# A decoder layer in 32-bit products: the border inside its second feed-forward, the loads ahead of its mixer's output, and its opening, ordered anew

## The chip, the cores and the metric

The kernel runs on one core of one Trainium2 chip. The metric is the time of one execution on the device in microseconds (us). The three runs of the kernel before lie within 0.62 us of each other.

## The reference

One layer of a decoder, batch 1, 1024 tokens and 16 meta tokens ahead of them, width 1024, feed-forward width 2816, all in float32. Cut to what matters:

```
h = h + 0.5 * swiglu(rms_norm(h, ffn1_norm), ffn1_w_in, ffn1_w_out)
u = rms_norm(h, mix_norm) @ w_in
o = concat(hgrn2(u[...]), stick_breaking(u[...]))
h = h + o @ w_out
h = h + 0.5 * swiglu(rms_norm(h, ffn2_norm), ffn2_w_in, ffn2_w_out)
return h without the padding and the meta tokens

def swiglu(h, w_in, w_out):
    g, u = split(h @ w_in, 2)
    return (silu(g) * u) @ w_out
```

## The kernel before

Every large product is made of three matmuls. A float32 operand is split into a rounded high part and the rest: ScalarE casts the high part (`wh`, `xh`, `th`), VectorE subtracts it from the source to get the low part (`wl`, `xl`, `tl`), and TensorE adds up high by high, low by high and high by low. The two feed-forwards save products besides, by Winograd's form of Strassen's scheme: operands are cut into two by two blocks, and sums and differences of blocks (operands T1 to T4 on the side of the activations, s1, s2 and so on the side of the weights) are multiplied instead of the blocks alone.

The stages run one after the other: first feed-forward in and out, row norm and projection `w_in`, the HGRN2 heads and the attention woven into each other, the product with `w_out` in two halves (first the half whose operand `oT` comes back from memory, `first_half_of_o`; then the half from `oH`), the row norm with its transposes ("turns"), and the second feed-forward in and out. TensorE's order is written out by hand (`manual_schedule`). The order on the other engines comes from a scheduler, which puts work under `high_priority` ahead and holds work under `issue_after(x)` until x has been issued. All loads are issued by SP, in one order; a load waits on SP for the tile it overwrites and for its queue lane (there are eight), and all loads behind it wait too. Pools are regions of the on-chip memory: a pool that opens where another was must wait for the last use of what lay there.

The product into the feed-forward is `fast_in` (from L255). For each pair of 128 feature columns it runs two quads (gate and up). A quad loads four weight blocks (`block`, L275), makes their sums on GpSimd, splits them (`operand`, L270 and L272) and does seven groups of twelve matmuls into the banks qa, qb, qc (L315), in the order B11, T2, B21, T3, T1, T4, B22 of the operands on the other side. The gate goes through Silu; gate times up is stored to memory as `act` (four blocks B11 to B22, L427), and GpSimd makes the four sums T1 to T4 from them (`combined`, L442 and L449) and stores them too. For the last pair of the second feed-forward `combined` is put aside in `self.late`.

The first 272 tokens of the first feed-forward don't go through Strassen's scheme: they are "plain" (banks qd), run first, while the other two thirds of the tokens are loaded, normed (`norm_rows`, L645 to L665), turned and made into operands (`first_block`, `first_combined`). That opening starts with the rows of x (L614 to L617), the squares on ScalarE (L660) and VectorE (L656), root, reciprocal, scaling (L661 to L665), the transposes (L642) and the plain operand X (L674, L675). VectorE and GpSimd also build masks there: a memset, two selects on GpSimd (L112, L116) and a cast (L120) per level, one `sd` tile for all levels.

The product out of the feed-forward is `fast_out` (from L486): seven steps (A12, A11, S1, S2, S4, S3, A22), each over eleven quarters q, each of twelve matmuls (L593). A quarter loads a block of w_out (`raw`, L503, 256 KB) and one of act (L508, 256 KB) through the pool `ring`, and splits both into the pool `parts` (L513 and L515, four buffers). After quarter 3 of A12 `load_h` loads the eight residual rows hN (512 KB each, L1772), into which the steps' results are added. At quarter 2 of A12 the hook `between` runs the late `combined`.

Between the two products of the second feed-forward, the pools wq and xs_b (operands T2, T3, T1, T4, B22 in that order, 16 KB a partition each) close, and ring, parts and h3 (hN) open in that order on the same memory, from the bottom up. So the ring (24 KB) lies over wq, which holds the split weight blocks, and the beginning of T2; parts (32 KB) lie over T2, T3 and the beginning of T1; hN over T1, T4 and B22.

Of the kernel before, what the change touches and what calls it, by code (L numbers as in the profile page):

```python
# [34 lines left out]
def drain(gen):  # L35
    for _ in gen:
        pass


class Block:  # L40
# [53 lines left out]
    def setup_rest(self, pool):  # L94
# [32 lines left out]
        nc.vector.tensor_sub(mx, l0, l1)  # L127
        nc.scalar.activation(self.lb, mx, AF.Sigmoid)
        nc.scalar.activation(self.lbc, mx, AF.Sigmoid, scale=-1.0)

# [124 lines left out]
    def fast_in(self, ops, n, w_in, actD, openers, ev0, open_ev, feed=None, plain=None,  # L255
# [71 lines left out]
        def plain_quad(col, take):  # L327
            for i in range(2):
                ps = None
                for h in range(2):  # L330
                    ps = alone(ps, operand(block(i, h, col)), h, h == 0)
                    if h == 1:
                        take(i, ps)
                    yield
# [65 lines left out]
        def pair(f, opened=None, also=(None, None)):  # L400
# [17 lines left out]
            def up(i, j, ps, plus):  # L418
                t = sg[i, j]
                if plus is None:  # L420
                    nc.vector.tensor_mul(t, ps, t)  # L421
                else:
                    u = ev["p"].tile([P, n], F32, tag="u", name="u", bufs=2)
                    nc.vector.tensor_add(u, ps, plus)
                    nc.vector.tensor_mul(t, u, t)
                if (i, j) != (0, 1):
                    nc.gpsimd.dma_start(actD[f // 2, f"B{i + 1}{j + 1}"], t)  # L427
                elif self.late is None or f // 2 < D_FF // 256 - 1:
                    combined()
                else:  # L430
                    self.late.append(combined)

            def combined():
# [11 lines left out]
                t1 = made(sg[0, 1], sg[0, 0])  # L445
                put("T1", t1)
                t2 = made(sg[1, 1], t1)
                put("T2", t2)
                sub(sg[0, 1], sg[1, 1], sg[0, 1])  # L449
                put("T3", sg[0, 1])  # L450
                put("T4", made(sg[1, 0], t2))

# [33 lines left out]
    def fast_out(self, out_of, n, w_out, actD, load_h, ready, between=lambda a, q: None,  # L486
# [90 lines left out]
        for bank, a, b, start, (i, j) in steps:  # L577
# [4 lines left out]
            for q in range(nq):  # L582
                with ExitStack() as first:
                    if a == "A12" and q < 2 and not plain:
                        first.enter_context(self.tc.high_priority())
                    wh, wl = halved(left(a, q), "w", 512)
                    xh, xl = halved(right((q, b), n), "t", n)
                order = [(m, e) for m in range(nb) for e in range(3)]
                if a == "A12" and q == 0:
# [162 lines left out]
    def hgrn_fill(self, xh, xl, pool, dst):  # L752

        nc = self.nc
        plan = [(kind, h) for h in range(4) for kind in "vfqg"]
        first = {"v": 1024, "f": 512, "q": 0, "g": 1536}
# [572 lines left out]
    def run(self):  # L1329
# [20 lines left out]
        with ExitStack() as c0:  # L1350
            with ExitStack() as c1:
                with tc.manual_schedule(engines={nc.tensor.engine}), ExitStack() as c2:
# [39 lines left out]
                    for _ in self.first_block(2, rows[1], rp, "ba", ops, ba):  # L1392
                        next(steps)
                    rows.append(self.rows_of(1, rp, nc.sync))
                    self.norm_rows(1, rows[2], junk)
                    drain(islice(steps, 4))
                    for _ in self.first_block(1, rows[2], rp, "bb", None, bb):
                        next(steps)
                    for _ in self.first_combined(ba, bb, ops, rp, nw):
                        next(steps)  # L1400
                    drain(steps)
# [199 lines left out]
            with tc.manual_schedule(engines={nc.tensor.engine}):  # L1601
                right, cx, pre = ExitStack(), ExitStack(), ExitStack()
                with ExitStack() as c1:
# [11 lines left out]
                    def from_dram(b):  # L1615
                        t = self.pool_o.tile([P, 2, 4, P], F32R, tag="oT", name="oT", bufs=3)
                        for i in range(2):
                            nc.sync.dma_start(
                                t.bitcast(F32)[:, i],
# [41 lines left out]

                    for b in range(2):
                        begin(0, b)
                    ws[1] = self.mix_weights(0, 1)
                    xa = self.pool("xs_a", ctx=right, side="right")
# [38 lines left out]
                    for at, (_, f) in enumerate(self.mix_out(  # L1704
# [5 lines left out]
                        if at % 4 == 3 and i:  # L1710
                            next(turns[b])
                            due.append((at + 7, turns[b]))
                        if due and due[0][0] <= at:
                            next(due.pop(0)[1])
                self.wq = self.pool("wq", ctx=cx)
                xb = self.pool("xs_b", ctx=cx)
                operands(xb, ("T2", "T3", "T1", "T4", "B22"))
                self.pin = self.pool("pin2", 1, PSUM, cx)
# [33 lines left out]
                cx.close()  # L1752
                with ExitStack() as c1:
                    self.ring = self.pool("ring", ctx=c1)
                    self.parts = self.pool("parts", ctx=c1)
                    self.pout = self.pool("pout2", 1, PSUM, c1)
                    hN = self.pool("h3", ctx=c1).tile([P, KT, D], F32, name="hN3")

# [10 lines left out]

                    def load_h():  # L1770
                        for b in range(KT):
                            nc.sync.dma_start(hN[:, b, :], h2N[b])  # L1772

                    def between(step, q):
                        if step == "A12" and q == 2:
                            self.late.pop()()
                            right.close()

                    self.op = lambda: self.pool("op", ctx=c1, side="right")
                    self.ring_bufs = 6  # L1780
                    self.fast_out(out_of, n, a["ffn2_w_out"][0], actD, load_h, ready, between)

# [22 lines left out]
```

## Time and profile before

| | us |
|---|---|
| median of 3 runs | 2097.42 (2096.95 to 2097.57) |
| the profiled execution | 2094.55 |
| its span | 2092.8 |
| TensorE busy in it | 2013.8 (96%) |
| VectorE busy | 1380.0 (66%) |
| ScalarE busy | 903.9 (43%) |
| GpSimd busy | 632.2 (30%) |
| mean granted TensorE clock | 0.993 |

In the profile PE is TensorE's matmuls and PEld its weight loads, DVE is VectorE, ACT ScalarE, POOL GpSimd, SP the engine that issues the loads. A row of the timeline has the start, the duration, the engine, the line of the kernel, the operation, what it writes and reads, how many in succession were merged (x2), and in brackets how long the engine was idle before and what released it. A granted clock below 1 means that TensorE ran at a lower speed in a part of the stretch.

### The profile page before, as it was taken

The numbers are of one execution on the slowest core, as the hardware profiler recorded it, in microseconds if no ns is written. First come the engines' busy times: TensorE is split into PE (matmuls) and PEld (weight loads), VectorE is DVE, ScalarE is ACT, GpSimd is POOL, SyncE is SP. The second block draws the span as 40 slices with busy tenths as digits, with TensorE's granted clock in tenths as the row PEclk, the third lists the DMA queues.
The fourth block names the chain that finished last, engine by engine and source line by source line (L and its number), as shares of the span: only waits on it lengthen the run. The fifth ranks groups of instructions, "written<-read, shape, count | busy, mean of one in ns | idle before, by whom it ended". The sixth has DMA issues, their size and how long they took to land.

```text
span 2092.8 us, 31593 instructions
## 1 busy us (share of the span) xinstructions
PE 2013.8 (96%) x11249; PEld 1788.4 (85%) x11249; DVE 1380.0 (66%) x2073; ACT 903.9 (43%) x1859; POOL 632.2 (30%) x692
## 2 busy tenths in 40 slices
PE   7999999999999999999999998999999999989998
PEld 6999999999987899988887887787788888867887
DVE  6867745556788832367788676558676676656874
ACT  7633333334564534356666515145233233224443
POOL 2256635442000002253333201112564454530000
PEclk9999999999999999999999999999999999999999
DMA  7643322327875636344444154763332332348563
GB/s 216 203 141 109 114 83 90 102 73 236 289 230 178 207 108 198 131 135 117 127 131 127 49 198 142 237 210 111 111 106 91 106 115 92 101 176 304 169 226 111
DMA packets 287534, 313.90 MB, mean 150 GB/s; under 512 B 24016, under 2 KB 215888, under 8 KB 287376
## 3 DMA queue, kind: packets, MB, share of 16 engines
q1 hardware_dynamic: 270192, 259.78, 39.9%
q0 software_dynamic: 16144, 52.10, 6.5%
q8 instruction: 89, 1.46, 0.3%
q14 instruction: 69, 0.57, 0.1%
q10 hardware_dynamic: 1040, 0.00, 0.0%
HBM read 227.57 MB, written 84.23 MB: 149 GB/s over the span
## 4 chain that ended last, share of the span: by engine, by line
PE 77%; DVE 5%; ACT 2%; DMA 2%; issue 2%; POOL 0%; SPq 0%; DVEq 0%; ACTq 0%; POOLq 0%
PE o L593 17%; PE qb L315 13%; PE qc L315 8%; PE qa L315 8%; PE proj L164 5%; PE proj L162 5%; PE proj L163 5%; PE qd L315 3%; PE o L556 3%; PE wo L1244 3%; PE flip L1063 2%; PE lvl L832 2%; DVE keep L1209 1%; PE oacc L1133 1%; PE oacc L1135 1%
## 5 line engine op out<-in xcount | busy, mean ns | idle before, releaser
L315 PE MATMUL qb<-T,wh 128*128 128x384 f32 (+1 forms) x1056 | 319.5, 363 | 6.9 <-DVE u L359 6.8
L272 DVE TENSOR_TENSOR wl<-s,wh 128x512 fp32r<-128x512 f32 x176 | 200.1, 1137 | 96.5 <-ACT wh L270 92.4
L315 PEld LDWEIGHTS qb<-T,wh 128*128 128x128 f32 x1056 | 195.8, 188 | 31.8 <-ACT wh L270 9.2
L593 PE MATMUL o<-wh,th 128*128 128x512 f32 x539 | 212.3, 396 | 9.7 <-ACT th L513 9.7
L315 PE MATMUL qa<-B,wh 128*128 128x384 f32 (+1 forms) x704 | 214.8, 367 | 2.2 <-DVE sg L421 1.4
L593 PE MATMUL o<-wl,th 128*128 128x512 f32 x539 | 211.2, 394 | 0.9 <-DVE wl L515 0.9
L593 PE MATMUL o<-wh,tl 128*128 128x512 f32 x539 | 211.1, 393 | 0.7 <-DVE tl L515 0.7
L272 DVE TENSOR_TENSOR wl<-raw,wh 128x512 fp32r<-128x512 f32 x184 | 172.2, 938 | 53.6 <-ACT wh L270 49.9
L162 PE MATMUL proj<-xh,wh 128*128 128x384 f32 (+2 forms) x576 | 204.9, 356 | 0.2 <-ACT xh L252 0.2
L270 ACT CAST wh<-s 128x512 fp32r<-128x512 f32 x176 | 109.3, 622 | 220.0 <-PE qb L315 171.4
L163 PE MATMUL proj<-xh,wl 128*128 128x384 f32 (+2 forms) x576 | 199.2, 346 | 0.0
L164 PE MATMUL proj<-xl,wh 128*128 128x384 f32 (+2 forms) x576 | 198.9, 345 | 0.1
L270 ACT CAST wh<-raw 128x512 fp32r<-128x512 f32 x184 | 113.4, 619 | 198.1 <-PE qc L315 106.6
L315 PE MATMUL qb<-T,wl 128*128 128x384 f32 (+1 forms) x528 | 191.9, 363 | 1.3 <-DVE wl L272 1.3
L513 ACT CAST th<-act 128x512 fp32r<-128x512 f32 (+2 forms) x176 | 96.8, 550 | 186.8 <-PE o L593 138.9
L315 PE MATMUL qd<-X,wh 128*128 128x272 f32 x704 | 146.3, 294 | 5.8 <-ACT wh L270 4.9
L515 DVE TENSOR_TENSOR tl<-act,th 128x512 fp32r<-128x512 f32 (+2 forms) x176 | 105.1, 600 | 64.8 <-ACT th L513 64.7
L315 PEld LDWEIGHTS qa<-B,wh 128*128 128x128 f32 x704 | 130.4, 188 | 19.2 <-DVE sg L421 1.8
L285 POOL TENSOR_TENSOR s<-raw 128x512 f32<-128x512 f32 x88 | 119.2, 1354 | 82.1 <-DVE wl L272 65.4
L1209 DVE TENSOR_TENSOR_SCAN keep<-keep 128x144 f32<-128x144 f32 (+6 forms) x112 | 127.2, 1138 | 8.3 <-ACT keep L1205 6.0
L1214 POOL TENSOR_TENSOR sig<-sig,keep 128x144 f32<-128x144 f32 (+3 forms) x64 | 88.1, 1377 | 141.8 <-DVE keep L1209 79.3
L315 PE MATMUL qa<-B,wl 128*128 128x384 f32 (+1 forms) x352 | 128.7, 366 | 0.4 <-DVE wl L272 0.4
(340 smaller groups left out, 4767.4 us busy)
## 6 DMA issues: line engine op xcount, KB each, us to landing
raw<-in_ffn_w_in_dram SPq DMA_DIRECT2D x224, 256.0 KB, 3.0
raw<-in_ffn_w_out_dram SPq DMA_DIRECT2D x176, 256.0 KB, 4.2
raw<-in_w_in_dram SPq DMA_DIRECT2D x28, 512.0 KB, 4.4
ks<-kD SPq DMA_DIRECT2D x32, 260.0 KB, 5.5
oT<-oD SPq DMA_DIRECT2D x32, 256.0 KB, 4.8
ak<-in_ffn_w_out_dram SPq DMA_DIRECT2D x22, 256.0 KB, 4.9
v<-vD SPq DMA_DIRECT2D x8, 576.0 KB, 4.7
vD<-vhl SPq DMA_DIRECT2D x8, 512.0 KB, 3.6
```

What stands on the lines that cost most here:

```text
L162: nc.tensor.matmul(ps, wh[:, s], xs, start=k == 0, stop=False)
L163: nc.tensor.matmul(ps, wl[:, s], xs, start=False, stop=False)
L164: nc.tensor.matmul(ps, wh[:, s], xl[:, k, c0 : c0 + n], start=False, stop=k == nk - 1)
L270: nc.scalar.copy(hi, src)
L272: nc.vector.tensor_sub(lo, src, hi.bitcast(F32))
L285: op(t, x, y)
L315: nc.tensor.matmul(ps, a[:, k, :], b[:, k0 + k, :], start=start and k == 0 and i == 0, stop=k == 3 and i == 2, skip_group_check=True,)
L513: nc.scalar.copy(hi, src)
L515: nc.vector.tensor_sub(lo, src, hi.bitcast(F32))
L593: nc.tensor.matmul(banks[bank][m], z[:, m * P : (m + 1) * P], y, start=start and q == 0 and e == 0, stop=q == nq - 1 and e == 2, skip_grou ...
L1209: nc.vector.tensor_tensor_scan(out=kv, data0=kv, data1=kv, initial=1.0 if last else keep[:, end : end + 1], op0=ALU.mult, op1=ALU.bypass,)
L1214: nc.gpsimd.tensor_mul(sig, sig, keep[:, 1 : nk + 1])
```

## The change

Six edits.

The operands of the second feed-forward are allocated in the order B22, T4, T1, T3, T2 instead of T2, T3, T1, T4, B22, so the ones read last lie lowest. The pools of the product out open in the order h3, parts, ring instead of ring, parts, h3: hN (32 KB a partition) comes to lie over wq and B22, a new tile `spare` (24 KB) over T4 and part of T1, parts (32 KB) over the rest of T1 and T3, the ring (24 KB) over T2 and free memory.

`load_h` does nothing there any more; the hook `between` issues one residual row at each of the quarters 3 to 10 of A12. `combined` yields after each of its sums; the late one is begun one sum at a time at the quarters 2 to 5, each behind a one-column copy on GpSimd (into `spare`) that reads the newest low part `tl`. Everywhere else it is drained at once.

In the mixer, the loads of the first two rows hm and of four blocks of w_out (`ws[1]`) are held until the last oT load has been issued. The turns of the norm come one k step (three matmuls) later.

In the opening, the plain quads' operands, with their loads, get high priority; the two sigmoids of the mixer's bounds move in the code to the HGRN2 heads; and the plain steps are dealt out among the other thirds' transposes in another rhythm.

```diff
@@ plain_quad
-                    ps = alone(ps, operand(block(i, h, col)), h, h == 0)
+                    with self.tc.high_priority():
+                        w = operand(block(i, h, col))
+                    ps = alone(ps, w, h, h == 0)
@@ up
-                    combined()
+                    drain(combined())
@@ combined: a yield behind put("T1"), put("T2") and put("T3")
@@ fast_out
+                self.newest = xl
@@ the opening
                     for _ in self.first_block(2, rows[1], rp, "ba", ops, ba):
-                        next(steps)
+                        drain(islice(steps, 2))
...
-                    drain(islice(steps, 4))
                     for _ in self.first_block(1, rows[2], rp, "bb", None, bb):
-                        next(steps)
-                    for _ in self.first_combined(ba, bb, ops, rp, nw):
-                        next(steps)
+                        drain(islice(steps, 2))
+                    for at, _ in enumerate(self.first_combined(ba, bb, ops, rp, nw)):
+                        if at % 5 < 4:
+                            next(steps)
@@ from_dram
-                            nc.sync.dma_start(
+                            self.last_o = nc.sync.dma_start(
@@ the mixer's second half
-                    for b in range(2):
-                        begin(0, b)
-                    ws[1] = self.mix_weights(0, 1)
+                    with tc.issue_after(self.last_o.ins):
+                        for b in range(2):
+                            begin(0, b)
+                        ws[1] = self.mix_weights(0, 1)
...
-                            due.append((at + 7, turns[b]))
+                            due.append((at + 8, turns[b]))
...
-                operands(xb, ("T2", "T3", "T1", "T4", "B22"))
+                operands(xb, ("B22", "T4", "T1", "T3", "T2"))
@@ the second product out
+                    ph = self.pool("h3", ctx=c1)
+                    hN = ph.tile([P, KT, D], F32, name="hN3")
+                    spare = ph.tile([P, 3, 2, D], F32, name="spare")
+                    self.parts = self.pool("parts", ctx=c1)
                     self.ring = self.pool("ring", ctx=c1)
-                    self.parts = self.pool("parts", ctx=c1)
                     self.pout = self.pool("pout2", 1, PSUM, c1)
-                    hN = self.pool("h3", ctx=c1).tile([P, KT, D], F32, name="hN3")
...
-                    def load_h():
-                        for b in range(KT):
-                            nc.sync.dma_start(hN[:, b, :], h2N[b])
+                    held = []
 
                     def between(step, q):
-                        if step == "A12" and q == 2:
-                            self.late.pop()()
+                        if step != "A12":
+                            return
+                        if q >= 3:
+                            nc.sync.dma_start(hN[:, q - 3, :], h2N[q - 3])
+                        if q == 1:
+                            held.append(self.late.pop()())
+                        if 2 <= q <= 5:
+                            mark = nc.gpsimd.tensor_copy(
+                                spare[:, 0, 0, q : q + 1], self.newest[:, 0:1].bitcast(F32)
+                            )
+                            with tc.issue_after(mark.ins):
+                                next(held[0], None)
+                        if q == 5:
+                            drain(held[0])
                             right.close()
```

**The border on SP.** Rows of SP from the first load of the second product out, with what each waits for; raw is a block of w_out, act one of the activations, hN a residual row, DMAHW and DMASW are queue lanes. Before:

```order
L503 DMA raw<-in_ffn_w_out_dram 128x512 [waits DVE_49,PE_49]
L503 DMA raw<-in_ffn_w_out_dram 128x512
L508 DMA act<-act0B_13833 128x512 [waits DMAHW5_49,DMASW6_49,Pool_49]
L508 DMA act<-act1B_13840 128x512 [waits DMAHW6_49,DMASW4_49]
L503 DMA raw<-in_ffn_w_out_dram 128x512 [waits DMAHW7_49]
L508 DMA act<-act2B_13847 128x512 [waits DMAHW0_49,DMASW3_49]
L503 DMA raw<-in_ffn_w_out_dram 128x512 [waits DMAHW1_49]
L508 DMA act<-act3B_13854 128x512 [waits DMAHW2_49,DMASW2_49]
L1772 DMA hN_19221<-h2N 128x1024 [waits DMAHW3_49,DMASW1_49,DMASW0_49]
L1772 DMA hN_19221<-h2N 128x1024 [waits DMAHW4_49]
```

Now:

```order
L506 DMA raw<-in_ffn_w_out_dram 128x512 [waits PE_49]
L506 DMA raw<-in_ffn_w_out_dram 128x512
L511 DMA act<-act0B_13833 128x512 [waits DMAHW5_49,DMASW6_49]
L511 DMA act<-act1B_13840 128x512 [waits DMAHW6_49,DMASW4_49]
L506 DMA raw<-in_ffn_w_out_dram 128x512 [waits DMAHW7_49,PE_49]
L511 DMA act<-act2B_13847 128x512 [waits DMAHW0_49,DMASW3_49]
L506 DMA raw<-in_ffn_w_out_dram 128x512 [waits DMAHW1_49]
L511 DMA act<-act3B_13854 128x512 [waits DMAHW2_49,DMASW2_49]
L1785 DMA hN_19212<-h2N 128x1024 [waits DMAHW3_49,DVE_49,PE_49]
L506 DMA raw<-in_ffn_w_out_dram 128x512 [waits DMAHW4_49]
L511 DMA act<-act4B_13861 128x512 [waits DMAHW5_49,DMASW1_49]
L1785 DMA hN_19212<-h2N 128x1024 [waits DMAHW6_49]
```

The first eight loads no longer wait for VectorE or GpSimd, and the residual rows, eight in a run before, stand one between each two blocks; the first of them carries the wait for the memory of B22.

**The mixer on SP.** Rows of SP up to the last oT load; res are rows of the residual, KB a block of the HGRN2 heads, raw here a block of w_out. Before:

```order
L1656 DMA hm<-hmN 128x1024
L1618 DMA oT<-oD 128x4x128
L907 DMA KB<-hg_g 128x1024
L1626 DMA res<-h1N 128x512
L1618 DMA oT<-oD 128x4x128 x3
L1656 DMA hm<-hmN 128x1024
L1626 DMA res<-h1N 128x512
L1618 DMA oT<-oD 128x4x128 x2
```

Now:

```order
L1624 DMA oT<-oD 128x4x128 x2
L913 DMA KB<-hg_g 128x1024
L1632 DMA res<-h1N 128x512
L1624 DMA oT<-oD 128x4x128 x2
L1632 DMA res<-h1N 128x512
L1624 DMA oT<-oD 128x4x128 x2
L1632 DMA res<-h1N 128x512
L1624 DMA oT<-oD 128x4x128 x2
L1662 DMA hm<-hmN 128x1024 x2
```

The hm rows, 512 KB each, have moved from between the oT loads to behind the last of them.

**The opening on VectorE.** Its rows from the second memset of the masks on; ss_x holds the sums of squares, row the rows of x. Before:

```order
L664 RECIPROCAL ss_x<-ss_x 128x1
L656 SCALAR_TENSOR_TENSOR junk_229,ss_x<-row 128x1024
L665 TENSOR_SCALAR row<-row,ss_x 128x1024
L664 RECIPROCAL ss_x<-ss_x 128x1
L99 CAST ident_b<-ident 128x128
L665 TENSOR_SCALAR row<-row,ss_x 128x1024
L120 CAST masks<-sd 128x128
```

Now:

```order
L99 CAST ident_b<-ident 128x128
L120 CAST masks<-sd 128x128
L107 MEMSET sd 128x128
L111 MEMSET sd 128x32x2
L120 CAST masks<-sd 128x128
L107 MEMSET sd 128x128
L111 MEMSET sd 128x16x4
L120 CAST masks<-sd 128x128
L107 MEMSET sd 128x128
L111 MEMSET sd 128x8x8
```

Two more rounds follow in the same way (a cast, two memsets, a cast, a memset), and only then the first reciprocal: five levels of the masks stand ahead of the norm's first step on VectorE, none before. On SP the first row there is now the load of eight blocks of ffn_w_in, ahead of the four loads of the first rows of x, which came first before.

More of the change, by code (lines that the diff above doesn't have):

```diff
@@ L127, in setup_rest @@
         nc.vector.tensor_sub(mx, l0, l1)
-        nc.scalar.activation(self.lb, mx, AF.Sigmoid)
-        nc.scalar.activation(self.lbc, mx, AF.Sigmoid, scale=-1.0)
     def weights(self, name, raw, split, ctx, on_vector=False):
@@ L446, in combined @@
                 put("T1", t1)
+                yield
                 t2 = made(sg[1, 1], t1)
                 put("T2", t2)
+                yield
                 sub(sg[0, 1], sg[1, 1], sg[0, 1])
                 put("T3", sg[0, 1])
+                yield
                 put("T4", made(sg[1, 0], t2))
@@ L754, in hgrn_fill @@
         nc = self.nc
+        nc.scalar.activation(self.lb, self.mx, AF.Sigmoid)
+        nc.scalar.activation(self.lbc, self.mx, AF.Sigmoid, scale=-1.0)
         plan = [(kind, h) for h in range(4) for kind in "vfqg"]
@@ L1780, in run @@
                     self.ring_bufs = 6
-                    self.fast_out(out_of, n, a["ffn2_w_out"][0], actD, load_h, ready, between)
+                    self.fast_out(out_of, n, a["ffn2_w_out"][0], actD, lambda: None, ready, between)
 NAMES = [
```

## The prediction

> **What bounds the kernel now.** I read the page first. Its first part says that TensorE is busy nearly throughout, so only time in which TensorE waits, or runs at half clock after a wait, can be won.
>
> ```profile
> span 2092.8 us, 31593 instructions
> PE 2013.8 (96%) x11249; PEld 1788.4 (85%) x11249; DVE 1380.0 (66%) x2073; ACT 903.9 (43%) x1859; POOL 632.2 (30%) x692
> ```
>
> The profiled execution took 2094.55 us, 1.75 more than its span and 2.87 less than the median of 2097.42; I make the sum against 2094.55 and add 2.87 at the end. Then the waits of TensorE, asked for in the stretches that the change touches. Columns: who waits for whom, total us, times, longest.
>
> ```profile
> PE xps L642 <- DVE ss_x L664: 8.9, 1, 8.9
> PE qd L315 <- ACT wh L270: 4.9, 1, 4.9
> ...
> PE wo L1244 <- DMA oT<-oD: 4.1, 2, 3.7
> PE turn L247 <- DVE xn L240: 1.2, 1, 1.2
> ...
> PE o L593 <- ACT th L513: 9.7, 2, 6.3
> ```
>
> The largest, 9.7, stands between the two products of the second feed-forward. Third, the same stretches by windows: length, busy time and count of PE, PEld, DVE, ACT and POOL, granted clock, DMA share, GB/s.
>
> ```profile
> 0.00:14.43 14.43, 4.61 (x25) 4.20 (x25) 7.05 (x24) 7.76 (x17) 5.44 (x10) 1.00 0.94 287
> 37.80:48.00 10.20, 5.21 (x23) 4.68 (x22) 6.45 (x17) 8.50 (x17) 0.00 (x0) 0.67 0.28 72
> 1340.00:1362.00 22.00, 17.86 (x90) 13.96 (x89) 8.57 (x18) 3.04 (x7) 2.16 (x4) 0.92 0.95 307
> 1428.00:1456.00 28.00, 24.56 (x105) 18.82 (x105) 27.49 (x41) 23.08 (x43) 5.85 (x5) 1.00 0.44 123
> 1845.00:1862.00 17.00, 17.00 (x76) 13.80 (x74) 7.57 (x11) 2.97 (x5) 2.94 (x4) 1.00 0.08 32
> 1862.00:1874.00 12.00, 5.68 (x14) 4.31 (x14) 9.80 (x10) 4.95 (x8) 7.30 (x8) 0.72 0.91 325
> 1874.00:1892.00 18.00, 14.58 (x53) 11.46 (x52) 5.50 (x10) 5.67 (x10) 0.00 (x0) 0.81 1.04 412
> ```
>
> In the 17 us before the border the DMA engines move 32 GB/s and ScalarE works 3 us; in the 12 us after it everything is wanted at once. Where the clock column is below 1, a half clock lasted twice (1 - clock) of the stretch: 6.7 us from 1862 on, 6.8 from 1874 on, 3.5 in 1340 to 1362, 6.7 in 37.8 to 48.
>
> **The border of the second feed-forward.** Its timeline:
>
> ```profile
> 1845.60 0.39 PE L315 MATMUL qb<-T,wh 128*128 128x512 f32 x1
> ...
> 1861.83 0.39 PE L315 MATMUL qc<-B,wh 128*128 128x512 f32 x1
> 1862.25 0.84 SPq L503 DMA_DIRECT2D raw<-in_ffn_w_out_dram  x2
> ...
> 1862.98 0.69 DVE L425 TENSOR_TENSOR sg<-u,sg 128x512 f32<-128x512 f32 x1
> ...
> 1864.94 0.62 ACT L513 CAST wh<-raw 128x512 fp32r<-128x512 f32 x1 [10.17 <-DMA raw<-in_ffn_w_out_dram]
> ...
> 1865.59 3.93 DVE L515 TENSOR_TENSOR wl<-raw,wh 128x512 fp32r<-128x512 f32 x2 [1.92 <-ACT wh L513]
> ...
> 1866.03 6.14 SPq L1772 DMA_DIRECT2D hN<-h2N  x8
> ...
> 1868.53 2.07 PE L593 MATMUL o<-wh,th 128*128 128x512 f32 x4 [6.32 <-ACT th L513]
> ...
> 1869.44 1.28 DVE L515 TENSOR_TENSOR tl<-act,th 128x512 fp32r<-128x512 f32 x2
> ...
> 1873.82 0.53 PE L593 MATMUL o<-wh,th 128*128 128x512 f32 x1
> ...
> 1874.13 0.33 SPq L503 DMA_DIRECT2D raw<-in_ffn_w_out_dram  x1
> ...
> 1884.45 0.62 ACT L513 CAST wh<-raw 128x512 fp32r<-128x512 f32 x1 [11.97 <-DMA raw<-in_ffn_w_out_dram]
> ...
> 1885.74 0.80 PE L593 MATMUL o<-wh,th 128*128 128x512 f32 x1 [3.42 <-ACT th L513]
> ```
>
> The ring lies over the split weights' pool, so the first load of the second product goes out at 1862.25, when the last matmul (1861.83) has read them. TensorE waits 6.32; its first twelve matmuls then take 5.29 (1868.53 to 1873.82), against twelve times 0.23 in the stretch before it (17.00 us for 76 starts is 0.224 each): 2.6 lost to the clock. Behind the fourth weight block SP issues eight residual rows of 512 KB, so the fifth block goes out at 1874.13 and its split starts at 1884.45: a second wait of 3.42, and of the 6.8 us of half clock some 5.4 fall behind 1885.74 and cost half, 2.7. Together 6.3 + 2.6 + 3.4 + 2.7 = 15.0.
>
> After the change the ring of loads lies over T2, whose last reads are the twelve matmuls from 1845.60 on, so they end near 1848.4, and the splits' pool lies over T1 and T3, free by about 1856.5. Four weight blocks and four act blocks (2 MB, 6.5 us at 325 GB/s) land by about 1856, through a DMA that was idle. ScalarE is idle too and has 8 casts of 0.62 to do, 5 us, by 1862. VectorE does not get there: its rows put the first wl behind the sg of 1862.98 (end 1863.67), so wl comes at 1864.3, a second wl follows, and tl at 1865.7. TensorE has four matmuls on wh and th (to 1863.0), waits 1.3, has four on wl (to 1865.3), waits 0.4. So 1.7 is left of 15.0. The second wait: at quarter q (2.73 us of work each) SP now sends one row of 512 KB, then 512 KB of weight and act: 1 MB, 3.2 us at 325, 2.5 at 412. Quarter 4 lands near 1865.5 and is wanted at 1874.8; each further one loses 0.5, so quarter 10 still comes 5 us early. Cover gone, this would cost the 6.1 of before. The four held sums cost VectorE: two wl took 3.93 beside GpSimd's sums, two tl 1.28 alone, so a sum holds VectorE some 1.3. One sum a quarter makes 1.28 + 1.3 = 2.6 of 2.73: hidden, barely; not hidden, 0 to 3 in all. Term: **-13.3**, between -9 (sums and one more wait exposed) and -15.
>
> The Trainium skill ("SBUF — State Buffer", section "SBUF: two separate sides") says that VectorE, with two operands in SBUF, and a GpSimd instruction take one pair of ports, and that the loser is blocked for the whole instruction; the 3.93 against 1.28 agrees, and by that rule the term is the same.
>
> **The loads ahead of the mixer's last oT.**
>
> ```profile
> 1349.16 0.43 SPq L1656 DMA_DIRECT2D hm<-hmN  x1
> ...
> 1351.14 3.02 SPq L1618 DMA_DIRECT2D oT<-oD  x3
> ...
> 1359.26 1.22 PE L1244 MATMUL wo<-wh,oT 128*128 128x512 f32 x2 [3.67 <-DMA oT<-oD]
> ```
>
> The oT that ends the 3.67 is issued at 1351.14 behind an hm of 512 KB, in a DMA at 0.95 share. The change sends hm and two w_out blocks, 512 KB more, behind the last oT: 1 MB out of the way, 1.7 us at 307 GB/s for each half. If only hm counts the wait is 2.0, if both 0.3; I take 0.9, since the DMA is full throughout. A wait that short has not cost the clock elsewhere (the stretch from 1428 has a granted 1.00 with TensorE idle 3.4 in all), so the 2.8 us of half clock after 1359.26 (1.4 lost) goes too. Before 4.1 + 1.4 = 5.5, after 0.9: **-4.6**, between -2 and -5.5. hm and the held blocks are wanted only when the half of w_out from oH runs, some 20 us later.
>
> **Turns one step later.** A step is three matmuls, 0.7 us, against the wait of 1.2 for xn: **-0.7**, between 0 and -1.4.
>
> **Operand pools reversed at the start of the second feed-forward.** VectorE is busy 27.49 of 28: splits and turns are the bound whatever lies where, and T2 now waits for the last row's norm, which its own cast came after anyway. **0**, between -1.5 and +1.5.
>
> **The opening.**
>
> ```profile
> 2.48 0.71 POOL L116 TENSOR_SCALAR_AFFINE_SELECT sd<-sd 128x128 f32<-128x128 f32 x1
> 2.65 6.49 SPq L277 DMA_DIRECT2D raw<-in_ffn_w_in_dram  x8
> 5.31 1.06 ACT L660 ACTIVATE junk<-row 128x1024 bf16<-128x1024 f32 x1 [2.52 <-DMA row<-in_x_dram]
> ...
> 8.03 0.75 DVE L665 TENSOR_SCALAR row<-row,ss_x 128x1024 f32<-128x1024 f32 x1
> ...
> 8.88 4.61 PE L642 MATMUL xps<-ident,row 128*128 128x128 f32 x24 [8.88 <-DVE ss_x L664]
> ...
> 10.36 2.74 POOL L112 TENSOR_SCALAR_AFFINE_SELECT sd<-sd 128x128 f32<-128x128 f32 x1 [7.17 <-DVE sd L111]
> ...
> 14.43 0.59 PE L315 MATMUL qd<-X,wh 128*128 128x272 f32 x1 [0.94 <-DVE X L675]
> ...
> 42.95 0.60 PE L315 MATMUL qd<-X,wh 128*128 128x272 f32 x1 [4.86 <-ACT wh L270]
> ...
> 91.62 0.34 PE L315 MATMUL qa<-B,wh 128*128 128x384 f32 x1
> ```
>
> High priority takes the plain splits' loads along: eight blocks of 256 KB now go out ahead of the first rows of x. 2 MB and the first row at 287 GB/s from about 2 us end near 11, where the first row was squared from 5.31 on: about 6 late. VectorE meanwhile does four more rounds of the masks ahead of the first reciprocal, each two selects of 0.71 and a cast and memsets on VectorE that hand over to each other, some 2.2 by estimate: from 3.4 to about 12.3, as late as the row itself. From the row's scaling (8.03) to the first plain matmul (14.43) it was 6.4 and stays so: 14 + 6.4 = 20.5, **+6.1**, bounds +4.5 and, with each select at 2.74, +20. What it buys: the plain splits no longer stand behind the blocks of the other thirds on ScalarE and VectorE, so the wait of 4.86 goes, and with it half of the 5.0 us of half clock after 42.95, 2.5: -7.4. The plain stretch ends with the qa of 91.62:
>
> ```profile
> 14.43:91.62 77.19, 70.88 (x528) 69.40 (x529) 62.93 (x135) 60.26 (x119) 15.40 (x22) 0.96 0.59 174
> ```
>
> VectorE's 63 us of work in it now have 71 instead of 77, and the rows of the other thirds come later, so I allow +0.3 of new waits. Term: **-1.0**, between -4 and +6.
>
> [...]
>
> The sums that are no longer made at once elsewhere (drain) change nothing.
>
> **Sum.** -13.3 - 4.6 - 0.7 + 0 - 1.0 = -19.6. 2094.55 - 19.6 = 2075.0 profiled, 2077.8 as a median.
>
> **Rivals.**
> The opening loses: the rows of x, late behind the weights, make TensorE wait again for the B operands near 91, or the masks run longer: net +5 to +8 there instead of -1, total -11 to -14, 2083.5 to 2086.5. For it: VectorE's 8 us of slack are all it has. Against: 4.86 and 2.5 are there to win. 0.17.
> The second border wait stays: residual rows between the blocks fill the DMA (3.2 us a quarter against 2.73) and with the late sums' stores the lead of 5 to 9 us is eaten. +6, 2084. Against: 412 GB/s were reached there. 0.08.
> The oT wait stays, since the backlog at 0.95 share is of other loads and stores. Then -0.5 instead of -4.6: 2082. 0.08.
> Slower: the opening's mask rounds at 2.74 a select. Five rounds of 6 us end near 33, the first plain matmul comes at 40, +18 net, about 2097; it decides from a first plain matmul later than 41, where nothing of the other 18.6 is left. Against it: a select took 0.71 when VectorE was quiet, and it is quiet there. 0.02, with another 0.02 for just about no change.
> The change doing nothing at all can't be: the rows of SP differ in all three places.
>
> **How the numbers follow.** Forecast 0.65 at 2077.8, its own terms within 2072 and 2082. The other cases reach up to 2086.5. Range 2071 to 2086.5; below it the bounds all at their best (1 in 20), above it border and opening failing together. Measurement tells about 0.2%, 4.2 us, from no change: faster by more 0.96, same 0.02, slower 0.02.
>
> **What would show it.** Right: the first w_out load near 1848 less what was won before, one wait of 1 to 2 for wl (VectorE) at the border instead of 6.3 for th, none of 3.4 after it, no granted clock below 1 there; oT's wait below 2; the first plain matmul near 20 and no 4.9 wait behind it; the first qa at 88 to 92. Wrong: a first qa after 96, a wait for th or wh in the border's quarters 4 to 10, or 3 us of oT.

## The result, and the profile after

The changed kernel takes 2080.35 us in the median of 4 runs (2077.59 to 2080.70); the kernel before took 2097.49 in the median of the 4 runs beside it (2096.95 to 2099.33). The ratio is 0.9914, 95% interval 0.9897 to 0.9931: 17 us less, where 19.6 had been forecast. The profiled execution took 2077.59 with a span of 2075.9, against a span of 2092.8: 16.9 less.

The waits of TensorE, in the same stretches as in the forecast (columns: who waits for whom, total us, times, longest):

```profile
PE xps L646 <- DVE ss_x L668: 15.9, 1, 15.9
PE qd L313 <- DVE X L679: 1.7, 1, 1.7
...
PE turn L245 <- DVE xn L238: 1.2, 1, 1.2
PE wo L1250 <- DVE res L1636: 0.7, 1, 0.7
PE wo L1250 <- POOL oH L964: 0.6, 1, 0.6
...
PE qa L313 <- DVE sg L421: 2.8, 1, 2.8
...
PE o L597 <- DVE wl L518: 1.2, 1, 1.2
```

At the border (last line) 1.2 us are left of 9.7. The oT line is gone. The wait before the first transposes has grown from 8.9 to 15.9, and the wait of 4.9 for wh behind it is gone. The wait for sg at the start of the second feed-forward has grown to 2.8; in the kernel before it was 1.4:

```profile
PE qa L315 <- DVE sg L421: 1.4, 1, 1.4
```

The windows (length, busy time and count of PE, PEld, DVE, ACT and POOL, clock, DMA share, GB/s):

```profile
1336.00:1358.00 22.00, 21.09 (x122) 17.47 (x121) 9.74 (x20) 4.17 (x10) 2.71 (x5) 1.00 0.85 260
...
1438.00:1452.00 14.00, 11.22 (x42) 8.64 (x41) 12.87 (x20) 10.19 (x20) 2.05 (x2) 0.88 0.30 94
...
1845.00:1862.00 17.00, 16.62 (x73) 13.33 (x71) 8.79 (x13) 6.54 (x12) 2.95 (x4) 1.00 0.53 174
1862.00:1874.00 12.00, 11.16 (x48) 8.91 (x49) 11.60 (x14) 3.73 (x6) 7.18 (x9) 1.00 0.94 348
1874.00:1892.00 18.00, 18.00 (x81) 14.92 (x80) 9.84 (x15) 8.42 (x14) 2.65 (x4) 1.00 1.04 408
```

The DMA's idle time ahead of the border is now used (174 GB/s where there were 32), and the clock stays at 1.00 through it. It now falls in another place, at the start of the second feed-forward (0.88 of 14 us, or 3.4 us at half). The timeline of the border after:

```profile
1846.81 0.82 SPq L506 DMA_DIRECT2D raw<-in_ffn_w_out_dram  x2
...
1855.09 1.14 ACT L516 CAST wh<-raw 128x512 fp32r<-128x512 f32 x2 [1.82 <-PE qc L313]
...
1860.55 1.07 PE L597 MATMUL o<-wh,th 128*128 128x512 f32 x4
1860.75 0.32 SPq L1785 DMA_DIRECT2D hN<-h2N  x1
...
1861.48 0.69 DVE L425 TENSOR_TENSOR sg<-u,sg 128x512 f32<-128x512 f32 x1
1862.09 1.29 DVE L518 TENSOR_TENSOR wl<-raw,wh 128x512 fp32r<-128x512 f32 x2
...
1862.83 1.19 PE L597 MATMUL o<-wl,th 128*128 128x512 f32 x4 [1.21 <-DVE wl L518]
...
1865.50 0.62 ACT L516 CAST wh<-raw 128x512 fp32r<-128x512 f32 x1 [6.14 <-DMA raw<-in_ffn_w_out_dram]
...
1869.65 2.07 DVE L518 TENSOR_TENSOR wl<-raw,wh 128x512 fp32r<-128x512 f32 x1 [0.21 <-ACT wh L516]
...
1869.86 1.29 POOL L442 TENSOR_TENSOR t<-sg,t 128x512 f32<-128x512 f32 x1
```

The first loads go out 14 us ahead of the first matmul that wants them, the casts begin at 1855.1, and the one wait left is for wl, which stands on VectorE behind the last sg. The fifth block is ready at 1865.5. A late sum on GpSimd stretches one split of VectorE from 0.68 to 2.07, and TensorE does not wait for that.

Where the 16.9 us came from is read by counting TensorE's matmuls, whose number is the same (11249), and taking the start of the same one in both profiles. The difference, after less before:

| from one point to the next (time in the profile before) | us |
|---|---|
| start of the span to 65, where the opening's matmuls are in the same order again | -2.3 |
| 65 to 1341, code that the change leaves alone but for the two sigmoids | +2.1 |
| 1341 to 1363, the oT loads | -5.2 |
| 1363 to 1394, the other half of w_out, first turns | +1.7 |
| 1394 to 1463, last turns, start of the second feed-forward | +2.1 |
| 1463 to 1892, the border | -13.6 |
| 1892 to the last matmul | 0.0 |
| last matmul to the end of the span | -1.7 |

The second and the last line are no work of the change that could be named: among the kernels below the second line lies between +1.1 and +7.0, and the last between -1.0 and -1.8. Nine of the experiments have one or two spells of half clock between 1073 and 1290, where the kernel before and the changed kernel have none.

### The profile page after: what moved, and what is told of

It is laid out like the page before. It is cut to its first block, busy times and chain, and to the rows that moved or that the text cites. A ratio compares the mean times of both kernels' runs of the same rounds, so it can differ in the third digit from the quotient of the medians.

```text
span 2075.9 us, 31597 instructions
## 1 busy us (share of the span) xinstructions
PE 2005.5 (97%) x11249; PEld 1782.6 (86%) x11249; DVE 1382.7 (67%) x2073; ACT 901.6 (43%) x1858; POOL 632.4 (30%) x696
## 4 chain that ended last, share of the span: by engine, by line
PE 77%; DVE 6%; ACT 2%; DMA 2%; issue 2%; POOL 0%; SPq 0%; DVEq 0%; ACTq 0%; POOLq 0%
PE o L597 17%; PE qb L313 13%; PE qc L313 8%; PE qa L313 8%; PE proj L160 5%; PE proj L162 5%; PE proj L161 5%; PE qd L313 3%; PE o L559 3%; PE wo L1250 3%; PE flip L1069 2%; PE lvl L838 1%; DVE keep L1215 1%; PE oacc L1139 1%; PE oacc L1141 1%
```

## The experiments

All but the eleventh start from the changed kernel. For each, what it gave at the place is the same count of matmuls, and the profiled time of a single execution is only given beside it.

**1. The operands in the old order.**

```diff
-                operands(xb, ("B22", "T4", "T1", "T3", "T2"))
+                operands(xb, ("T2", "T3", "T1", "T4", "B22"))
```

> The changed kernel with one edit undone: the second feed-forward's operands lie in the old order again (T2, T3, T1, T4, B22), so the ring of loads comes to lie over B22, which is read last. Theory (the early ring is what removed the first wait at the border): the first w_out load goes out only after the last matmul of the product in, TensorE waits some 5.5 to 6.5 us for th or wh there and loses 2 to 3 more at half clock, 7 to 8 at this place in all. Rival (the residual rows one by one and the late sums removed it, the order of the pools is indifferent): the wait at the border stays at 1.2 us. For the start of the product in: if the reversed order is what made the wait for sg there 2.8 us (1.4 before), it goes back to about 1.4 and the half clock goes, 2 to 3 us won; if it comes from elsewhere, it stays at 2.8. Profiled time by the theory: 4 to 6 us above that of the changed kernel, 2082 to 2084; by the rival 2075 to 2078.

TensorE's waits at the start and at the border, and the first load at the border:

```profile
PE qa L313 <- DVE sg L421: 2.8, 1, 2.8
...
PE o L597 <- ACT th L516: 5.8, 1, 5.8
```

```profile
1864.37 0.85 SPq L506 DMA_DIRECT2D raw<-in_ffn_w_out_dram  x2
```

2087.91 in one run. The border is worth 7.1 instead of 13.6: the first load waits for the last reads again, and the wait for th of the kernel before is back. So the reversed order is what makes the early loads possible, worth 6.5. The whole is above the 2082 to 2084 that I gave: the stretches that this edit leaves alone came out longer in this profile, 65 to 1341 by 1.5 us alone. The wait for sg stays 2.8 in the old order: the pools did not make it.

**2. The residual rows in a run.**

```diff
-                        if q >= 3:
-                            nc.sync.dma_start(hN[:, q - 3, :], h2N[q - 3])
+                        if q == 3:
+                            for b in range(KT):
+                                nc.sync.dma_start(hN[:, b, :], h2N[b])
```

> The changed kernel, but all eight residual rows are issued in a run at quarter 3, as before. Theory (the second wait, in front of quarter 4, came of 4 MB of rows ahead of the fifth block): the fifth block lands 12 us after the rows start, near 1873 to 1875, TensorE waits 2 to 4 us for th in quarter 4 and loses up to 2.7 at half clock: 2 to 6 us more than the changed kernel. Rival (the four quarters loaded early are cover enough, the rows could stay in a run): no wait there, 0 us more.

2086.67 in one run. ScalarE waits for the fifth block, TensorE for its cast:

```profile
1878.23 0.62 ACT L516 CAST wh<-raw 128x512 fp32r<-128x512 f32 x1 [17.18 <-DMA raw<-in_ffn_w_out_dram]
...
1879.42 0.80 PE L597 MATMUL o<-wh,th 128*128 128x512 f32 x1 [4.33 <-ACT th L516]
```

The border is worth 6.5: 7.1 less, a little above the range given, since the fifth block came later than I had worked out. Four quarters of cover are not enough for 4 MB.

**3. The opening undone.** High priority, rhythm of steps and the place of the sigmoids as before.

> The changed kernel with the whole opening undone (no high priority for the plain quads, the old rhythm of steps, the sigmoids at their old place). Theory (the opening lost 7 us before the first plain matmul and won 9 behind it): the first plain matmul back at 14.4, the wait of 4.9 for wh near 38 and its half clock back, the first qa near 91.6 instead of 89.4: 2 us more than the changed kernel. Rival (the opening wins more downstream, in the first feed-forward): 4 us or more. Second rival (it wins nothing): 0 or less.

```profile
PE xps L647 <- DVE ss_x L669: 8.9, 1, 8.9
PE qd L315 <- ACT wh L270: 4.9, 1, 4.9
```

2081.50 in one run. From 65 to the end of the plain stretch TensorE is 1.4 us behind the changed kernel. The opening wins little, as the theory had it.

**4. High priority for the splits alone.**

```diff
-                    with self.tc.high_priority():
-                        w = operand(block(i, h, col))
+                    src = block(i, h, col)
+                    with self.tc.high_priority():
+                        w = operand(src)
```

> The changed kernel, but in the plain quads only the splits have high priority; their loads don't, so the rows of x are loaded first again and the masks' rounds stand behind the norm on VectorE again. Theory (the late first matmul comes of the loads that the priority takes along, the gain behind it of the splits): the first plain matmul at 14 to 15 us instead of 21.9, none of the 4.9 us wait for wh near 38, first qa at 82 to 84 instead of 89.4: 5 to 7 us less than the changed kernel, about 2074 as a median. Rival (the plain loads have to be early too, or a wait for wh or wl comes back behind the rows of the other thirds): first matmul at 14 to 15, but 4 to 8 us of waits for wh between 25 and 60: within 2 us of the changed kernel.

2081.94 in the median of 5 runs (2078.87 to 2090.18), ratio to before 0.9936, interval 0.9914 to 0.9958: no better than the changed kernel. The waits of TensorE, and what VectorE waited for:

```profile
PE xps L647 <- DVE row L670: 4.5, 1, 4.5
```

```profile
32.52 1.23 DVE L661 SCALAR_TENSOR_TENSOR junk<-row 128x1024 uint8<-128x1024 f32 x1 [1.18 <-DMA row<-in_x_dram]
```

TensorE starts 6.5 us earlier and has lost all of it again by 38 us, in front of the transposes of the second group of rows, one row of which is loaded by 32.5. The first qa comes at 89.16, not at 82 to 84. My theory was wrong: with the splits' priority kept, an earlier first matmul wins nothing, since TensorE then waits for that row.

**5. The turns one step earlier again, and 6. only the last of them.**

```diff
-                            due.append((at + 8, turns[b]))
+                            due.append((at + 7, turns[b]))
...
-                            due.append((at + 8, turns[b]))
+                            due.append((at + (8 if b < 6 else 7), turns[b]))
```

> The changed kernel with the turns one step earlier again (at + 7). Theory (the later turn of block 6 pushes its four differences on VectorE behind the start of the second feed-forward, and that is what made the wait for sg there 2.8 us and dropped the clock): the wait goes back to about 1.4, the granted clock there to 1.00, 2.5 to 3.5 us won at the start, 0 to 0.7 lost in the turns: 2 to 3 us less than the changed kernel. Rival (the held hm rows, which come later, made it): the wait stays at 2.8, and the time is 0 to 1 us longer than the changed kernel's.

> The changed kernel with block 6 alone turned at + 7 and all others at + 8. Theory: the wait for sg at the start of the second feed-forward goes back to about 1.4 as with all at + 7, and the turns keep what + 8 won: 2.5 to 3.5 us less than the changed kernel, the fastest of the versions so far, about 2077.5 as a median. Rival (the lag of all the turns counts, not of the last): the wait stays above 2.4, no difference.

The wait for sg in the fifth, and the window in the sixth:

```profile
PE qa L313 <- DVE sg L421: 1.4, 1, 1.4
```

```profile
1438.00:1452.00 14.00, 12.38 (x52) 9.40 (x51) 14.00 (x19) 11.79 (x22) 5.39 (x4) 1.00 0.39 115
```

From 1394 to 1463 both take as long as the kernel before (0.0 and -0.4), where the changed kernel takes 2.1 more. So the later turn of block 6 is what made the wait, and one step for that block alone takes it away. Not all of the 2.1 is the wait: experiments 2 and 10 have the same wait of 2.8 with the clock at 1.00, and lose 0.5 to 0.8 there. The medians, 2079.02 (4 runs, ratio 0.9917, 0.9901 to 0.9934) and 2079.43 (4 runs, 0.9918, 0.9903 to 0.9932), cannot be told from the changed kernel's: what was won there was not seen in the whole.

**7. The loads ahead of oT not held.**

```diff
-                    with tc.issue_after(self.last_o.ins):
-                        for b in range(2):
-                            begin(0, b)
-                        ws[1] = self.mix_weights(0, 1)
+                    for b in range(2):
+                        begin(0, b)
+                    ws[1] = self.mix_weights(0, 1)
```

> The changed kernel without the hold: the first two rows hm and the four w_out blocks are issued among the oT loads again. Theory (1 MB ahead of the last oT loads made the wait): the wait for oT is back, 3.5 to 4.5 us in two, with 1.4 at half clock, 4.5 to 5.5 us more at this place. Rival (the oT loads came in time for another reason, the KB or residual loads): no wait above 1 us.

```profile
PE wo L1250 <- DMA oT<-oD: 2.6, 1, 2.6
```

2079.80 in one run. The wait is back, 2.6 long, less than the 3.5 to 4.5 I expected and without half clock; from 1341 to 1363 it costs 2.5 us against the changed kernel. But the three waits of the changed kernel behind it (xn 1.2, res 0.7, oH 0.6) are gone, and from 1341 to 1394 this kernel is 0.8 us ahead of the changed one. What the hold wins at oT, the next waits take. Those for res and oH, 0.2 to 0.7 each, stand in every kernel with the hold and in none without it. The one for xn does not follow the hold: it is 1.2 long in the kernel before too, and gone in experiment 3, which has the hold.

**8. The late sums at once.** All four at quarter 2, without the copies.

```diff
-                        if q == 1:
-                            held.append(self.late.pop()())
-                        if 2 <= q <= 5:
...
+                        if q == 2:
+                            drain(self.late.pop()())
                             right.close()
```

> The changed kernel with the four late sums all at quarter 2, without the copies that hold them. Theory (a sum holds VectorE up for 1.3 us, and there is slack enough in the quarters): the same sums hold three or four splits in quarters 1 to 3, where the lead on TensorE is smallest: 0.3 to 1.5 us more at the border. Rival (the sums were a main cause of the first wait): 3 us or more. Second rival (indifferent): below 0.2.

```profile
PE o L597 <- DVE tl L518: 3.8, 1, 3.8
PE o L597 <- DVE wl L518: 1.2, 1, 1.2
```

```profile
1867.11 2.38 DVE L518 TENSOR_TENSOR wl<-raw,wh 128x512 fp32r<-128x512 f32 x2
1869.40 4.03 DVE L518 TENSOR_TENSOR tl<-act,th 128x512 fp32r<-128x512 f32 x2
```

```profile
1869.79 1.27 POOL L442 TENSOR_TENSOR t<-sg,t 128x512 f32<-128x512 f32 x1
1871.01 1.26 POOL L451 TENSOR_TENSOR sg<-sg 128x512 f32<-128x512 f32 x1
```

```profile
1874.00:1886.00 12.00, 12.00 (x45) 9.74 (x44) 7.16 (x11) 4.53 (x8) 2.04 (x2) 0.82 1.04 413
```

2089.43 in one run; the border is worth 7.2, 6.4 less. I expected 0.3 to 1.5, and the rival was right. GpSimd here starts the sums as soon as the last sg is done (the first at 1867.3), though the code names quarter 2, so they meet the very first two quarters' splits, where there is no lead at all; a second wait of 3.8 appears, and behind it the clock falls to 0.82 over 12 us.

**9. No priority, and 10. the old rhythm with priority.** The ninth takes `high_priority` out of `plain_quad`; the tenth has the steps before.

> The changed kernel without the high priority in the opening, with the new rhythm of steps. Theory (what binds the opening up to some 45 us is the norm and the transposes of the second group of rows on VectorE and ScalarE, not the first matmul): first plain matmul at 14.4, then a wait of 3 to 5 us in front of a transpose or a split between 25 and 42, and by 62 us TensorE is within 1 us of the changed kernel. Rival (the priority itself is what won): the old wait of 4.9 for wh near 38 is back, and TensorE is 1.5 to 3 us behind the changed kernel at 62. Second rival (the early loads were pure loss): 4 to 7 us ahead at 62.

> The changed kernel with the high priority, but the old rhythm of steps. Theory (the old rhythm asks for the second group's transposes eight steps earlier, while their norm stands behind the prioritised splits): a wait for row of 4 to 8 us in front of the transposes near 30, TensorE 1 to 5 us behind the changed kernel at 62. Rival (the rhythm is indifferent): within 0.5 us at 62.

The ninth's waits:

```profile
PE qd L313 <- DVE wl L270: 3.2, 4, 2.2
```

The tenth's:

```profile
PE xps L646 <- DVE ss_x L668: 15.8, 1, 15.8
PE qd L313 <- DVE X L679: 2.2, 1, 2.2
PE qd L313 <- ACT sp L392: 1.2, 1, 1.2
```

At 65 us in the profile before, the ninth is 0.3 behind the changed kernel, and 2.0 at the end of the plain stretch, since it loses 1.7 more between 70 and 74; the tenth is 1.4 behind at both (2085.97 and 2079.92 in one run each). The ninth's first matmul at 14.4 wins nothing, as the theory said: a wait of 2.2 for wl at 37.7, with 3.4 us of half clock, and shorter ones behind it take the lead back. But 62, where I meant to judge, was too early: by the end of the plain stretch the priority is worth 2.0 in these profiles. The tenth's rhythm costs 1.4, mainly by a wait of 1.2 for sp and not by the one for row that I named.

**11. The border alone**, on the kernel before.

> The kernel before with the border's edits alone (reversed pools, residual rows one by one, late sums held); opening, loads ahead of oT and turns as before. Theory (the border wins 13 of the 17 us, and the start of the second feed-forward is not touched by the pools' order): 12.5 to 14 us won between the last matmul of the product in and quarter 5, the wait for sg at the start stays at 1.4, the waits of 8.9, 4.9 and oT stay: 2081.5 profiled, 12 to 14.5 us less than before as a median. Rival (the reversed pools cost 2 us or more at the start): 10 to 11.5 us less, and a wait for sg of 2.8.

```profile
PE wo L1249 <- DMA oT<-oD: 2.6, 1, 2.6
...
PE qa L315 <- DVE sg L422: 1.4, 1, 1.4
...
PE o L598 <- DVE wl L519: 1.2, 1, 1.2
```

2081.79 in the median of 4 runs (2077.30 to 2083.65), ratio 0.9925, 0.9904 to 0.9947; 13.6 won from 1463 to 1892. The wait for sg is 1.4. That is 13.6 at the place, as expected, and 15.4 by the medians, a little above the 12 to 14.5 given. By the medians the border alone is 15 of the 17 us, and what the other edits add is within the intervals.

**12. What was learned, together.** Block 6 turned at + 7, and in quarter 1 of A12 the first four matmuls ahead of quarter 0's other eight, so TensorE has 1.8 us of work instead of 0.9 before it needs a wl.

```diff
+                if a == "A12" and not plain:
+                    if q == 0:
+                        order, waiting = order[:nb], order[nb:]
+                    elif q == 1:
+                        order = order[:nb] + waiting + order[nb:]
```

> The changed kernel with block 6 turned at + 7, and with the high by high matmuls of quarter 1 of A12 put ahead of quarter 0's other eight. Theory (what is left at the border is the first wl behind the last sg on VectorE, 1.2 us, and the start's wait for sg is the last turn's): the wait for wl falls to 0.3 to 0.6, the wait for sg to 1.4 with no half clock: 3 to 4 us less than the changed kernel at these two places in the profile; as a median 2076 to 2078. Rival (what is won at one place is taken back downstream, as at the oT loads): both waits gone, but the median within 1 us of the changed kernel's 2080.35.

```profile
PE wo L1256 <- ACT oH L969: 2.4, 1, 2.4
...
PE qa L313 <- DVE sg L421: 1.4, 1, 1.4
...
PE o L603 <- DVE wl L518: 0.3, 1, 0.3
```

2076.76 in the median of 6 runs (2074.36 to 2078.24), ratio 0.9904, 0.9889 to 0.9920: the fastest version measured, though its interval overlaps that of the changed kernel. The border is worth 14.6, and the start 0.0 instead of +2.1. The wait for oH of 2.4 and 6.8 us of half clock that go with it (0.76 from 1370 to 1384) take back what the oT loads gave: of 5.2 won by 1363, 0.1 is left at 1394. The two waits and the median came as forecast, and the rival is out.

## Why the prediction was right, and where it was not

The time (2080.35 for 2077.8 forecast) was right mainly by its largest term; several smaller steps were not.

**The border, -13.3.** Measured -13.6 in the changed kernel and in the eleventh experiment alone. The steps hold one by one: the first load at 1846.8, which is the 1848 said less the 1.5 won before; a wait of 1.2 for wl (1.3 forecast), none for a block, no clock below 1. Experiments 1, 2 and 8 show that it takes all three edits: without any one of them 6.4 to 7.1 come back. What I had not seen is that the third one matters. I priced the held sums at 1.3 of VectorE in a quarter and called them hidden, which they are (wl took 2.07 beside a sum and nobody waited); but I did not price what they would do unheld, early loads given. The 1.3 a sum is confirmed: in experiment 8 two tl took 4.03 beside two sums, and 1.28 alone in the kernel before.

The Trainium skill's rule of the one pair of ports ("SBUF — State Buffer", section "SBUF: two separate sides") agrees with these rows in that a split is held for about the length of a sum (1.39 for one of 1.29). Which of the two took the ports first, on which the rule turns, they do not show: the split of 2.07 starts 0.2 before its sum by the rows, and is the one held up.

**The loads ahead of oT, -4.6.** At the place, 5.2. But the step "hm and the held blocks are wanted only 20 us later" stopped short: I did not ask what is late next. Of the 5.2, 1.7 were gone by 1394 in the changed kernel, 5.1 in experiment 12, and experiment 7 without the hold was no later there. Over 1341 to 1394 the eleven kernels with the hold won 2.5 in the mean (4.0 to 0.1), the two without it and the kernel before 4.3, 1.1 and 0. What the hold is worth in the end could not be told from nothing. The sum had it as 4.6 of 19.6, and booked the whole price of one wait without the waits behind it.

**Turns, -0.7, and the start of the second feed-forward, 0.** Neither came as forecast. The wait for xn is 1.2 long as before; with the turns at + 8 it lies between nothing and 1.7 in the profiles, so what the step does to it could not be told. The start lost 2.1, out of the bound of 1.5, by a wait of 2.8 and 3.4 us at half clock; where the clock stayed up (experiments 2 and 10) it lost 0.5 to 0.8, inside the bound. I looked for its cause in the pools and named VectorE, 27.49 of 28 busy, as the bound; then work moved within that stretch has to be priced too, and the turn I moved by a step issues four differences on VectorE. Experiment 1 clears the pools; 5 and 6 show that it was the turn of block 6. That turn also won 1.0 ahead of 1430, which the loss behind it outweighs.

**The opening, -1.0.** Measured -2.3 (1.4 by experiment 3). The parts: first plain matmul at 21.93 (20.5 forecast, +7.5 for +6.1), the wait of 4.9 gone, the first qa at 89.35, within the 88 to 92 given.

```profile
10.07 0.23 DVE L120 CAST masks<-sd 128x128 uint8<-128x128 f32 x1 [0.85 <-POOL sd L116]
...
12.03 1.06 ACT L664 ACTIVATE junk<-row 128x1024 bf16<-128x1024 f32 x1 [9.20 <-DMA row<-in_x_dram]
...
15.86 4.32 PE L646 MATMUL xps<-ident,row 128*128 128x128 f32 x24 [15.86 <-DVE ss_x L668]
...
21.93 0.39 PE L313 MATMUL qd<-X,wh 128*128 128x272 f32 x1 [1.75 <-DVE X L679]
...
89.35 0.34 PE L313 MATMUL qa<-B,wh 128*128 128x384 f32 x1
```

The masks were done at 10.3 and held nothing up; the row, squared from 12.03, was what was late. Between these two kernels both sides of the sum are there, each larger than I had it: 7.5 lost up to the first plain matmul, 9.8 won from there to the first qa (77.19 us before, 67.42 now). That they come out near my -1.0 is partly luck. The half clock did not simply go with the wait of 4.9, as the sum had it: 3.4 us of it now stand at 23 (0.84 from 19 to 30), where there were 6.7 from 41 on. And the 6.1 is no price that could be had back: experiments 3, 4 and 9 start 6.5 to 7 us earlier and stand level by 38 to 51 us, each behind another wait, for wh (4.9), for row (4.5) and for wl (2.2). The slower rival (mask selects of 2.74 in these rounds) did not come: the longest from 3 to 10 us took 0.54. The place of the two sigmoids was only undone together with the rest, in experiment 3, so its own share is open.

**What no step held.** +2.1 in code that the change leaves alone but for the two sigmoids (the eleventh experiment, with these at their old place, has +3.6 there) and -1.7 behind the last matmul: together 0.4. The chances of the cases, written down one by one, add up to 1.02, a slip.

## What to carry to other kernels

Where one product follows another on the same memory, lay the pool of the next one's first loads over what the last one reads first, and look at everything that queues behind them: the early loads, the rows spread and the sums held won 13.6 us together, and only 6.5 to 7.2 with any one of the three missing. When a wait goes, look for the second wait within a few microseconds behind it before its price is booked; here 1.7 to 5.1 of the oT loads' 5.2 us were lost again within the next 30 us. On an engine that is busy all through a stretch, moving a step by one place is not free: here one turn's four differences made a wait of 1.4 into one of 2.8.

## What the runs showed of the hardware

A wait shorter than the 3.4 us that a spell at half clock lasted here can go with a fall of the clock, and the same wait need not. With the wait of 2.78 for sg the changed kernel ran 3.4 us at half (clock 0.88 over 14 us); in experiments 2 and 10 the same wait left it at 1.00, and so did a wait of 1.4 there in experiments 5 and 6. Experiment 2's window:

```profile
1438.00:1452.00 14.00, 10.92 (x46) 8.19 (x46) 13.90 (x19) 10.85 (x20) 5.23 (x4) 1.00 0.38 114
```

A little later two waits of 1.8 and 0.9 dropped it in experiment 7 and not in the changed kernel. Their windows, the changed kernel's and then experiment 7's:

```profile
1452.00:1475.00 23.00, 19.43 (x84) 15.18 (x83) 11.95 (x17) 6.63 (x11) 10.27 (x8) 1.00 0.23 69
```

```profile
1452.00:1475.00 23.00, 19.84 (x73) 14.99 (x72) 11.22 (x16) 6.01 (x10) 9.66 (x8) 0.85 0.23 69
```

0.85 of 23 us is 6.9 at half; by the count of matmuls experiment 7 lost 2.7 more there than the changed kernel. In the forecast I had taken the clock as lost only by waits of 3.4 and more, from the four that the profile before showed. The Trainium skill ("TensorE: Matmul & The Clock Gate", section "Part 1: The HAM clock gate") puts the fall behind an idle window of about 3.4 us that runs freely; the 2.78 here is shorter, so by this measurement less than such a window of unbroken waiting can be enough. What decides between a fall and none at the same wait is open.

The stretch from 65 to 1341 us, the same code in all kernels but for the place of the two sigmoids, differed from the kernel before by +1.1 to +7.0 us from one profile to the next, with waits of 0.5 to 1 us that came and went. Differences below about 4 us were to be had only at the place, by the count of matmuls, not from the whole.
